# A two-layer streaming encoder step: the two MLPs begin in a fixed engine order, the up product runs by halves of the tokens

## The chip, the cores and the metric

The kernel runs on one core of a Trainium2 chip. The core has a matrix engine (TensorE, PE in the profile, with its weight loads as PEld), three engines for elementwise work (VectorE = DVE, ScalarE = ACT, GpSimd = POOL) and SyncE (SP), which here only issues DMAs. Each engine runs its own list of instructions in order and waits on semaphores. The metric is the device time of one execution in microseconds.

## The reference

Two layers run over 1072 tokens (16 meta, 32 sample and 1024 prompt tokens) of width 1024, in fp32. Layer 0 mixes by windowed attention and gated linear attention, layer 1 by forgetting attention; what matters here is the end of each layer:

```python
def rmsnorm(x, g):
    xf = x.astype(jnp.float32)
    y = xf * lax.rsqrt(jnp.mean(xf * xf, axis=-1, keepdims=True) + EPS)
    return (y * g.astype(jnp.float32)).astype(x.dtype)

def mlp(h, w_up, w_down):
    u = jax.nn.relu(h @ w_up)
    return (u * u) @ w_down
...
    xp = xp + mlp(rmsnorm(xp, norm_mlp[l]), w_up[l], w_down[l])
    xs = xs + mlp(rmsnorm(xs, norm_mlp[l]), w_up[l], w_down[l])
```

The hidden width is 4096, so w_up is 1024 x 4096 and w_down 4096 x 1024.

## The kernel before, in words

**Residual and products.** The residual stream stands transposed in SBUF: `xT` is [128, 8, 1072], feature block by token. It is cut into four quarters of tokens (268 wide in layer 0, 264 in layer 1). An fp32 product is done as three matmuls (`mm3`, L72 to L77): every operand is split by `hi_lo` (L62) into a high part, a cast on ScalarE (L64), and a low part, a subtraction on VectorE (L66). The mixer's output product (`add_product`, L823) adds 8 feature blocks of each quarter to `xT` (L833).

**Norm.** Beside these products `norm` squares the quarter on ScalarE (L134), adds the squares on VectorE and Pool (L136, L139), takes the column mean with one matmul by a constant matrix (L145) and forms the reciprocal root on ScalarE and VectorE (L148 to L152). `mlp_norm` (L867) scales `xT` by gain and root in 8 VectorE instructions (L873).

**MLP operands.** The up product is done with seven products in place of eight on 2 x 2 blocks. The blocks are B11, B21 (quarters 0 and 1, upper and lower features), B12, B22 (quarters 2 and 3) and the sums T1 to T4 (`mlp_sums`, L879), and each is split into `ho_B` or `ho_T` tiles. Halves c = 0 and 1 are the first and the second quarter of such a pair. The weights go by 16 column pairs b; for each, `up_load` (L899) fetches 1 MB of w_up into `mu_raw`, and `up_weights` (L907) forms the seven pieces A11 to S4 (`mu_w`).

**Up.** `up` (L932) runs, for each b, the seven pieces in the order of `UP` (L896), both halves with one piece: A11 with B11, A12 with B21, S1 with T1, S2 with T2, S3 with T3, A22 with T4, S4 with B22. One piece in one half is a step of 12 matmuls. The results are evicted into `xT`'s own memory (`xT` itself is first saved to `xsave` in HBM), squared, combined by four subtractions (L1000) and stored as `ud` by one DMA on SP's queue (L1001). Two areas of `xT` take turns, so pair b + 2 overwrites what pair b stored.

**Down.** `down` (L1010) runs seven passes in two halves over 16 blocks kb. It loads four 1 MB pieces of w_down (`md_k`, L1018) and reads `ud` back in pieces (`md_ur`, L1058), which are split into `md_w` and `md_u`. In the first pass `xT` is restored from `xsave` (L1102); one-element Pool copies (L1064) keep such loads from starting before a given activation piece has been read.

**Order.** In the MLP only TensorE's list is written by hand; VectorE, ScalarE, Pool and SP are ordered by a scheduler that follows a simulated timeline. Pools of tiles lie in two stacks, left and right; a tile that lies where an earlier one lay waits for that tile's last use.

## Time and profile before

| | us |
|---|---|
| median of three runs | 2867.91 (2854.82, 2867.91, 2869.13) |
| the profiled execution, first to last | 2855.66 |
| its span, first to last instruction | 2853.9 |
| mean granted clock of TensorE | 0.963 |
| layer 0: first product add to steady up matmuls | 559.5 to 646.6 |
| layer 0: last up matmul, first down matmul | 972.67, 986.29 |
| layer 1: first product add to steady up matmuls | 2091.5 to 2164.2 |
| layer 1: last up matmul, first down matmul | 2485.25, 2499.10 |

The times are taken from one profiled execution. A row of a timeline is start, duration, engine, line, operation, output<-inputs, shape, and in brackets the idle time ahead of it and what ended that. In a row of a group stand the number of instructions, busy time and mean duration. Durations of neighbours overlap by their start-up, so the distance between starts is the shorter and the truer cost.

### The profile page before, as it was taken

To read this page: it belongs to the slowest core of one execution; us is meant where nothing else is said; L and a number is where in the kernel's file an instruction comes from. 1 tells how busy PE (TensorE), PEld (TensorE's weight loads), DVE (VectorE), ACT (ScalarE), POOL (GpSimd) and SP (SyncE) were. 2 spreads that over 40 slices of the span, in tenths; PEclk is the share of its full clock that TensorE was granted. 3 is DMA by queue.
4 is the path that set the end of the run, shared out by engine and by line. 5 is a ranking of instruction groups with operands and counts; after the bars stand their busy time and mean duration, and the time that the engine had idled before them with its cause. 6 is when DMAs were issued, how large, how long until landed. Compare 5 with 4: busy or idle time off the path is not lost.

```text
span 2853.9 us, 49119 instructions
## 1 busy us (share of the span) xinstructions
PE 2631.2 (92%) x18391; PEld 2440.6 (86%) x18391; DVE 1888.3 (66%) x3856; ACT 1264.4 (44%) x2820; POOL 560.7 (20%) x611
## 2 busy tenths in 40 slices
PE   5899988879999899999999978999978999899998
PEld 5788966769999799999789856778768999899998
DVE  5934376687676677578643556778888666677553
ACT  4435454243333345445333346666653333335342
POOL 3423354200000010003110244555520000010000
PEclk9999988899999899999999979999988999999999
DMA  5343241143445577544465374344332444486643
GB/s 192 100 134 104 72 140 45 30 120 101 151 129 164 202 231 218 168 134 121 123 193 168 115 176 127 89 101 102 77 91 79 144 147 144 164 274 205 200 138 105
DMA packets 371286, 393.77 MB, mean 138 GB/s; under 512 B 41503, under 2 KB 300280, under 8 KB 369000
## 3 DMA queue, kind: packets, MB, share of 16 engines
q1 hardware_dynamic: 368552, 383.62, 45.6%
q0 software_dynamic: 2496, 7.01, 0.7%
q8 instruction: 145, 2.38, 0.4%
q14 instruction: 93, 0.76, 0.1%
HBM read 263.94 MB, written 125.48 MB: 136 GB/s over the span
## 4 chain that ended last, share of the span: by engine, by line
PE 63%; issue 16%; DVE 9%; DMA 3%; ACT 2%; SPq 1%; POOL 1%; DVEq 0%; ACTq 0%; POOLq 0%
PE bank L75 11%; PE bank L76 11%; PE bank L77 11%; PE mu_y L77 5%; PE mu_y L76 5%; PE mu_y L75 5%; PE bank L1470 2%; PE bank L1480 1%; PE bank L1481 1%; PE fx_s L1452 1%; PE fx_s L1453 1%; DMA md_raw<-in_w_down 1%; PE bank L257 1%; DVE gl_Q L600 1%; PE b L701 1%
## 5 line engine op out<-in xcount | busy, mean ns | idle before, releaser
L75 PE MATMUL bank<-pj_wh,h 128*128 128x384 f32 (+3 forms) x832 | 298.0, 360 | 9.4 <-ACT pj_wh L64 7.0
L77 PE MATMUL bank<-pj_wh,h 128*128 128x384 f32 (+3 forms) x832 | 295.9, 357 | 6.0 <-DVE h L66 4.8
L76 PE MATMUL bank<-pj_wl,h 128*128 128x384 f32 (+3 forms) x832 | 297.3, 358 | 3.5 <-DVE pj_wl L66 3.5
L75 PE MATMUL mu_y<-md_u,md_w 128*128 128x268 f32 (+1 forms) x896 | 259.4, 289 | 26.9 <-ACT md_u L64 26.9
L76 PE MATMUL mu_y<-md_u,md_w 128*128 128x268 f32 (+1 forms) x896 | 257.8, 288 | 2.4 <-DVE md_u L66 2.4
L77 PE MATMUL mu_y<-md_u,md_w 128*128 128x268 f32 (+1 forms) x896 | 257.3, 287 | 0.0
L75 PE MATMUL bank<-md_u,md_w 128*128 128x268 f32 (+1 forms) x896 | 257.1, 287 | 0.0
L77 PE MATMUL bank<-md_u,md_w 128*128 128x268 f32 (+1 forms) x896 | 255.2, 285 | 0.0
L76 PE MATMUL bank<-md_u,md_w 128*128 128x268 f32 (+1 forms) x896 | 254.9, 285 | 0.0
L64 ACT CAST md_u<-md_ur 128x536 fp32r<-128x536 f32 (+1 forms) x224 | 141.1, 635 | 210.7 <-PE mu_y L77 110.7
L66 DVE TENSOR_TENSOR md_u<-md_ur,md_u 128x536 fp32r<-128x536 f32 (+1 forms) x224 | 157.9, 710 | 114.2 <-ACT md_u L64 113.8
L76 PE MATMUL mu_y<-ho_T,mu_w 128*128 128x268 f32 (+1 forms) x768 | 219.8, 286 | 0.2 <-DVE ho_T L66 0.2
L77 PE MATMUL mu_y<-ho_T,mu_w 128*128 128x268 f32 (+1 forms) x768 | 219.9, 286 | 0.0
L75 PE MATMUL mu_y<-ho_T,mu_w 128*128 128x268 f32 (+1 forms) x768 | 219.2, 285 | 0.0
L75 PEld LDWEIGHTS mu_y<-md_u,md_w 128*128 128x128 f32 x896 | 171.1, 191 | 27.4 <-ACT md_u L64 27.3
L66 DVE TENSOR_TENSOR mu_w<-mu_raw,mu_w 128x512 fp32r<-128x512 f32 x160 | 110.0, 688 | 117.0 <-ACT mu_w L64 117.0
L1283 POOL TENSOR_TENSOR fx_p<-fx_p,sm_den 128x144 f32<-128x144 f32 (+7 forms) x128 | 150.6, 1177 | 181.8 <-DVE sm_den L1282 164.7
L64 ACT CAST mu_w<-mu_raw 128x512 fp32r<-128x512 f32 x160 | 99.2, 622 | 188.6 <-PE bank L77 124.6
L75 PEld LDWEIGHTS bank<-pj_wh,h 128*128 128x128 f32 x832 | 158.8, 191 | 22.3 <-ACT pj_wh L64 7.5
L76 PEld LDWEIGHTS mu_y<-md_u,md_w 128*128 128x128 f32 x896 | 170.9, 191 | 3.5 <-DVE md_u L66 3.4
L77 PEld LDWEIGHTS bank<-pj_wh,h 128*128 128x128 f32 x832 | 158.6, 191 | 17.5 <-DVE h L66 5.1
L76 PEld LDWEIGHTS bank<-pj_wl,h 128*128 128x128 f32 x832 | 159.0, 191 | 16.3 <-DVE pj_wl L66 5.2
(538 smaller groups left out, 8096.2 us busy)
## 6 DMA issues: line engine op xcount, KB each, us to landing
md_raw<-in_w_down SPq DMA_DIRECT2D x160, 256.0 KB
mu_raw<-in_w_up SPq DMA_DIRECT2D x64, 512.0 KB
ud<-xT SPq DMA_DIRECT2D x16, 1876.0 KB
md_ur<-ud SPq DMA_DIRECT2D x112, 268.0 KB
ud<-xT SPq DMA_DIRECT2D x16, 1848.0 KB
md_ur<-ud SPq DMA_DIRECT2D x112, 264.0 KB
md_k<-in_w_down SPq DMA_DIRECT2D x16, 1024.0 KB
fh_ka<-zk SPq DMA_DIRECT2D x32, 260.0 KB
```

What stands on the lines that cost most here:

```text
L64: nc.scalar.copy(hi, src)
L66: nc.vector.tensor_tensor(lo, src, hi.bitcast(F32), op=ALU.subtract)
L75: mm(out, ah, bh, start=start, stop=False)
L76: mm(out, ah, bl, start=False, stop=False)
L77: mm(out, al, bh, start=False, stop=stop)
L257: nc.tensor.matmul(*args, start=k == x == 0, stop=k == KB - 1 and x == 1)
L600: eng.tensor_tensor(ov, xv[r, :, :, 1], qv[r, :, :, 1], op=ALU.mult)
L701: nc.tensor.matmul(po[:m, h % 2, h // 2], att[:, h, :m], v[:, P * h:P * h + P], start=True, stop=False)
L1283: nc.gpsimd.tensor_tensor(p[:, :n], p[:, :n], den[:, 0:1].to_broadcast([P, n]), op=ALU.mult)
L1452: nc.tensor.matmul(s[:, a:b], qa[:, qc], ka[:, t0 + a:t0 + b], start=True, stop=False)
L1453: nc.tensor.matmul(s[:, a:b], qb[:, qc], kb[:, t0 + a:t0 + b], start=False, stop=ma >= mb)
L1470: nc.tensor.transpose(pt[:m, P * j:P * j + P], pr[j][:, k0:k0 + m], self.ident)
```

## The change

**Begin of the MLP.** `mlp_start` replaces `norm`, `mlp_norm` and `mlp_sums` for the MLPs. It writes out one order for TensorE, VectorE and ScalarE (`in_order`): after each product it squares the block on ScalarE, saves two blocks at a time, and lets `beside` emit queued work (weights, scalings, operand forms) until a budget of estimated us is used. The square sums are halved by two pair additions a quarter, and the column sums are accumulated by TensorE (two matmuls after each). `xT` is scaled by the root alone, in two instructions of four blocks; the gains go into the up weights (`up_gain`, ScalarE).

**Up.** The 32 units (b, c) follow each other in an order that interleaves two units. `mlp_first` emits its first steps in the fixed order too, until the last operand is formed; behind that only TensorE's list is fixed. Evictions use strided places in `xT`; A22's square goes from VectorE to ScalarE; the `ud` store goes from SP's queue to Pool's.

**Down.** The first w_down load and the first activations come ahead of the other loads, six weights are formed ahead instead of sixteen, and the pools are cut finer.

**Memory.** The stacks of many tiles change sides, so that operands and weights of the MLP lie where they wait for other tiles than before. In `scaled`, the norm of the few first rows takes two `nm_t` tiles in place of one `lx_t` tile, a buffer that the loads of x use as well.

```diff
+            for k0 in range(0, KB, 4):
+                t0 = sb.tile([P, w], F32, name="nm_t", bufs=bufs)[:, :4 * few].rearrange("p (k f) -> p k f", f=few)
+                for k in range(4):
+                    nc.vector.scalar_tensor_tensor(t0[:, k], x[:, k0 + k, :few], self.gain[:, n, k0 + k:k0 + k + 1], y[:, :few], op0=ALU.mult, op1=ALU.mult)
+                self.hi_lo(t0, h[:, k0:k0 + 4, 0:few], h[:, k0:k0 + 4, 64:64 + few])
...
+        self.up_pool = pool
+        self.operands("ho1", [(x, c) for c in range(2) for x in ("B11", "B21")])
+        self.nst = pool("nst")
+        self.operands("ho2", [(x, 0) for x in ("T2", "T1", "T3")])
+        self.mua = pool("mua")
...
+        self.scales = 0
+        self.raw0, self.w0 = self.up_load(0, self.mua), {}
+        for k in range(0, KB, 2):
+            self.work.append((0.4, lambda k=k: [self.up_gain(self.raw0, k + j) for j in range(2)], None))
+        for x in ("A11", "A12", "S1", "S2", "S3"):
+            self.work.append((1.0, partial(self.up_weights, x, self.raw0, self.w0), None))
...
+    def in_order(self):
+        return self.tc.manual_schedule(engines={mybir.EngineType.PE, mybir.EngineType.DVE, mybir.EngineType.Activation})
...
+    def beside(self, us):
+        self.step += 1
+        for f in self.due.pop(self.step, ()):
+            f()
+        while self.work and us > 0 and self.work[0][2] in (None, *self.ho):
+            t, f, _ = self.work.popleft()
+            f()
+            us -= t
+    def later(self, steps, f):
+        self.due.setdefault(self.step + steps, []).append(f)
...
+        def form(q, y):
+            c0, c1 = self.qs[q]
+            x1, x2 = (self.xT[:, k:k + 4, c0:c1] for k in (0, 4))
+            yb = y.unsqueeze(1).to_broadcast([P, 4, qw])
+            def scale(x, *then):
+                def go():
+                    self.scales -= 1
+                    tt(x, x, yb, op=ALU.mult)
+                    for name in then:
+                        hi(name, x, q)
+                return 1.25, go, None
+            def low(name, x):
+                return 1.25, lambda: lo(name, x, q), (name, q % 2)
+            def sub(dst, a, b, name=None):
+                def go():
+                    tt(dst, a, b, op=ALU.subtract)
+                    if name:
+                        hi(name, dst, q)
+                    else:
+                        self.formed.add(("free", q))
+                return 1.25, go, None
+            def high(name, x):
+                return 0.0, lambda: hi(name, x, q), (name, q % 2)
+            if q < 2:
+                return [scale(x1, "B11"), scale(x2, "B21"), low("B11", x1), low("B21", x2)]
+            a0, a1 = self.qs[q - 2]
+            b11, b21 = (self.xT[:, k:k + 4, a0:a1] for k in (0, 4))
+            return [scale(x1), sub(b11, x1, b11, "T1"), scale(x2), low("T1", b11), sub(b11, x2, b11, "T2"), sub(x1, x2, x1, "T3"),
+                    low("T2", b11), sub(b21, b21, b11), low("T3", x1), high("T4", b21), high("B22", x2), low("T4", b21), low("B22", x2)]
+        sums, pairs = {}, {}
+        def column_sums(q, n):
+            if n == 0:
...
+                sums[q] = self.ps.tile([P, 512], F32, name="mu_y")
+            sq = pairs.pop((q, n))
+            for j in range(2):
+                nc.tensor.matmul(sums[q][:, :qw], self.mean, sq[:, j], start=n == j == 0, stop=n == j == 1)
+        def row(q):
+            ps = sums.pop(q)
+            while self.scales:
+                self.work.popleft()[1]()
+            y, a = (sb.tile([P, QMAX], F32, name=f"ns_{x}")[:, :qw] for x in "ya")
+            nc.scalar.activation(a, ps[:, :qw], AF.Ln, bias=self.eps)
+            nc.scalar.activation(y, a, AF.Exp, scale=-0.5)
+            nc.scalar.activation(a, y, AF.Square)
+            def finish():
+                nc.vector.scalar_tensor_tensor(a, ps[:, :qw], EPS, a, op0=ALU.add, op1=ALU.mult)
+                nc.vector.scalar_tensor_tensor(y, a, -3.0, y, op0=ALU.add, op1=ALU.mult)
+                self.work.extend(form(q, y))
+                self.scales = 2
+            self.later(1, finish)
+        for q in range(4):
+            c0, c1 = self.qs[q]
+            for ob in range(KB):
+                product(q, ob)
+                n = ob // 4
+                if ob % 4 == 0:
+                    sq = []
+                if ob % 2 == 0:
+                    sq.append(sb.tile([P, 2, QMAX], F32, name=f"ns_q{len(sq)}", bufs=2 - len(sq))[:, :, :qw])
+                nc.scalar.activation(sq[ob % 4 // 2][:, ob % 2], self.xT[:, ob, c0:c1], AF.Square)
+                if ob % 2:
+                    nc.sync.dma_start(self.xsave[:, ob - 1:ob + 1, c0:c1], self.xT[:, ob - 1:ob + 1, c0:c1])
+                if ob % 4 == 3:
+                    pairs[q, n] = sq[0]
+                    self.later(2, lambda a=sq[0], b=sq[1]: tt(a, a, b, op=ALU.add))
+                    self.later(3, partial(column_sums, q, n))
+                    if n:
+                        self.later(3, partial(row, q))
+                self.beside(us)
...
+    def up_load(self, b, pool):
+        raw = pool.tile([P, KB, 2, P], F32, name=f"mu_raw{b % 2}", bufs=1)
...
             self.nc.sync.dma_start(raw[:, :, h], wu[:, :, h, P * b:P * b + P])
...
+    def up_gain(self, w, k):
+        x = w["raw"][:, k]
+        self.nc.scalar.mul(x, x, self.gain[:, 2 * self.l + 1, k:k + 1])
...
+        units = [(b, c) for b in range(self.NP) for c in range(2)]
+        order = [(0, "A11"), (0, "A12"), (0, "S2"), (0, "S1"), (0, "S3")]
+        for u in range(len(units)):
+            late = [(u + 1, "A11"), (u, "A22"), (u + 1, "A12"), (u, "S4"), (u + 1, "S2"), (u + 1, "S1"), (u + 1, "S3")]
+            order += [x for x in late if x[0] < len(units)]
...
-        def ready(at):
-            for b, n in todo[at:at + 4]:
-                if (b, n) not in ws:
-                    if b not in pairs:
-                        pairs[b] = {"raw": self.up_load(b, sb)}
-                    ws[b, n] = self.up_weights(self.UP[n][0], pairs[b], sb)
...
+        raws, ws, pr = {0: self.raw0}, {0: self.w0}, {}
+        def load(b):
+            raws[b] = self.up_load(b, self.mub if b % 2 else self.mua)
+        load(1)
+        for u, wn in order:
+            b, c = units[u]
+            yield 1.2, ((self.UP[wn], c), wn)
+            w = ws[b][wn]
+            at = self.qs[2 * (b % 2)][0]
...
+            if c:
+                def squared(x):
+                    stt(v[x], v[x], 0.0, v[x], op0=ALU.max, op1=ALU.mult)
+                if wn == "A12":
+                    squared("B11")
...
+                    squared("B22")
                 elif wn == "A22":
-                    nc.scalar.activation(u["B21"], out, AF.Relu)
+                    nc.scalar.activation(v["B21"], v["B21"], AF.Square)
                 elif wn == "S4":
-                    tt(u["B12"], u["B12"], out, op=ALU.add)
...
-            elif wn == "S4":
-                squared(v["B12"], v["B12"])
-                for x, p, m in (("T1", "B12", "B11"), ("T2", "B22", "T1"), ("T3", "B22", "B12"), ("T4", "B21", "T2")):
-                    tt(v[x], v[p], v[m], op=ALU.subtract)
-                nc.sync.dma_start(self.ud[b // 4][:, b % 4], place[:, b % 2, 1:8, :hw])
...
+                    squared("B12")
+                    for x, p, m in (("T1", "B12", "B11"), ("T2", "B22", "T1"), ("T3", "B22", "B12"), ("T4", "B21", "T2")):
+                        tt(v[x], v[p], v[m], op=ALU.subtract)
+                    nc.gpsimd.dma_start(self.ud[b // 4][:, b % 4], place[:, 1:8])
...
+                if b + 1 < self.NP:
+                    if wn == "A11":
+                        ws[b + 1] = {}
+                        for k in range(KB):
+                            self.up_gain(raws[b + 1], k)
+                    for x in {"S2": (), "S1": ("S1", "S2")}.get(wn, (wn,)):
+                        self.up_weights(x, raws[b + 1], ws[b + 1])
...
-        for kb in range(NP):
+        load(k1[0], "A11", 0, 4)
+        ready(0)
+        for x in range(1, 4):
+            load(k1[x], "A11", 4 * x, 4)
+        for kb in range(6):
             w[0, kb] = weights(0, kb)
...
+                if n == 0 and c == 0 and kb + 6 < NP:
+                    w[0, kb + 6] = weights(0, kb + 6)
...
+                ks = ExitStack()
+                kp = pool(ks, "mk", "right")
...
+                k2, k1 = ([kp.tile([P, 4, 512], F32, name=f"md_k{x}{y}") for y in range(4)][::-1] for x in (2, 1))
+                if self.l:
+                    self.so = pool(st, "so", "left", 2)
+                sb = {x: pool(st, f"md{x}") for x in ("u", 0, 1, 2, 3, "raw")}
...
+    def mlp_first(self):
+        self.operands("ho3", [(x, 1) for x in ("B22", "T4", "T3", "T1", "T2")] + [(x, 0) for x in ("B22", "T4")], "right")
+        self.mub = self.up_pool("mub", "right")
+        for x in ("A22", "S4"):
+            self.work.append((1.0, partial(self.up_weights, x, self.raw0, self.w0), None))
+        self.steps = self.up()
+        for us, wants in self.steps:
+            while not all(x in self.formed or x in self.w0 for x in wants):
+                self.beside(0.1)
+            if us:
+                self.beside(us)
+            if ("B22", 1) in self.formed and not self.work:
+                break
...
-            norm()
+            first.close()
...
-            steps = [[partial(product, q, ob) for ob in range(KB)] for q in range(4)]
-            for q in range(4):
-                while steps[q]:
-                    steps[q].pop(0)()
-                self.spill(q)
-                if q < 3:
-                    self.mlp_norm(q, [steps[q + 1].pop(0) for _ in range(3)])
+            with self.in_order():
+                self.mlp_begin(1)
+                self.mlp_start(product, 1.5)
+        with self.in_order():
+            self.mlp_first()
...
+            for n in range(2):
+                load(n)
+            for n in range(2):
+                split(n)
...
+                C.mlp_start(product, 1.0)
+        with C.in_order():
+            C.mlp_first()
```

VectorE's list in layer 1, quarter 3, from the last root of the norm to the operands; before (`ho_T_2381x` and `ho_B_23815` are operands with both halves in one tile):

```order
L152 SCALAR_TENSOR_TENSOR nm_y<-nm_a,nm_y 128x264
L873 SCALAR_TENSOR_TENSOR xT<-xT,gain,nm_y 128x264 x8
L884 TENSOR_TENSOR xT<-xT 128x4x264
L66 TENSOR_TENSOR ho_B_23815<-xT,ho_B_23815 128x4x264
L888 TENSOR_TENSOR xT<-xT 128x4x264
L66 TENSOR_TENSOR ho_T_23811<-xT,ho_T_23811 128x4x264
L66 TENSOR_TENSOR ho_T_23813<-xT,ho_T_23813 128x4x264
L886 TENSOR_TENSOR xT<-xT 128x4x264
L890 TENSOR_TENSOR xT<-xT 128x4x264
L66 TENSOR_TENSOR ho_T_23812<-xT,ho_T_23812 128x4x264
```

Here the products are over; the scalings are eight instructions with the gain, and all forms follow. After, the same place in quarter 2, where the last products run (L827 adds a product to `xT`, L977 adds a pair of squares):

```order
L958 SCALAR_TENSOR_TENSOR ns_y<-ns_a,ns_y 128x264
L911 TENSOR_TENSOR xT<-xT,ns_y 128x4x264
L921 TENSOR_TENSOR xT<-xT 128x4x264
L827 TENSOR_TENSOR xT<-xT,bank 128x264
L911 TENSOR_TENSOR xT<-xT,ns_y 128x4x264
L900 TENSOR_TENSOR ho_T_23557<-xT,ho_T_23557 128x1056
L827 TENSOR_TENSOR xT<-xT,bank 128x264
L977 TENSOR_TENSOR ns_q_23885<-ns_q_23885,ns_q_23913 128x2x264
L921 TENSOR_TENSOR xT<-xT 128x4x264 x2
L827 TENSOR_TENSOR xT<-xT,bank 128x264
L900 TENSOR_TENSOR ho_T_23556<-xT,ho_T_23556 128x1056
```

The scalings are two instructions of four blocks each, the forms stand between product adds, and the first T operands have tiles of one half.

SP's list at layer 0's change from up to down, before (`mu_raw` is the last up weights, `ud` the store, `md_k` the first w_down loads, `md_ur` the activations):

```order
L903 DMA mu_raw<-in_w_up 128x8x128 x2
L1001 DMA ud_6543<-xT 128x3752 x2
L1018 DMA md_k_10197<-in_w_down 128x4x512
L1018 DMA md_k_10198<-in_w_down 128x4x512
L1018 DMA md_k_10199<-in_w_down 128x4x512
L1018 DMA md_k_10200<-in_w_down 128x4x512
L1058 DMA md_ur<-ud_6540 128x2x268 x2
L1058 DMA md_ur<-ud_6541 128x2x268
```

The w_down loads stand ahead of the activations and behind a `ud` store. After:

```order
L992 DMA mu_raw_9829<-in_w_up 128x8x128 x2
L1163 DMA md_ur<-ud_6546 128x2x268 x2
L1163 DMA md_ur<-ud_6547 128x2x268 x2
L1163 DMA md_ur<-ud_6548 128x2x268
L1211 DMA xT<-xsave_5941 128x2x268 x2
L1163 DMA md_ur<-ud_6548 128x2x268
L1123 DMA md_k_10319<-in_w_down 128x4x512
L1123 DMA md_k_10318<-in_w_down 128x4x512
```

The activations and the first restore of `xT` stand ahead of the w_down loads, and the `ud` store is no longer in SP's list.

312 lines of the change are left out of this document (127 added, 185 removed).

## The prediction

> **What bounds the kernel now.** I read the page's busy line first, then the waits of TensorE, then the windows around the two longest waits, then the timeline there.
>
> ```profile
> PE 2631.2 (92%) x18391; PEld 2440.6 (86%) x18391; DVE 1888.3 (66%) x3856; ACT 1264.4 (44%) x2820; POOL 560.7 (20%) x611
> PE mu_y L75 <- ACT md_u L64: 26.9, 2, 13.6
> PE bank L75 <- ACT ho_T L64: 22.1, 2, 11.6
> 2163.80:2485.50 321.70, 321.70 (x2627) 321.53 (x2627) 221.40 (x383) 109.22 (x233) 0.00 (x0) 0.99 0.43 133
> 643.70:972.80 329.10, 326.94 (x2628) 326.35 (x2628) 225.85 (x386) 110.67 (x234) 0.00 (x0) 0.99 0.41 131
> 2091.50:2163.80 72.30, 39.05 (x252) 36.64 (x251) 65.02 (x126) 34.64 (x65) 9.02 (x8) 0.80 0.35 104
> 559.50:643.70 84.20, 61.52 (x440) 57.45 (x438) 70.09 (x133) 39.06 (x74) 7.91 (x8) 0.92 0.40 118
> ```
>
> The window rows give bounds, length, then busy PE, PEld, DVE, ACT, POOL, clock, DMA share, GB/s. TensorE is busy 92%, so only its idle time and its slow clock can be won. The two steady up stages (321.7 and 329.1 us) are TensorE alone, with VectorE a third idle; nothing in the change shortens them. Two waits, each met once in each layer, make 49 us: the start of the down stage (md_u) and the last operands of the up stage (ho_T). Ahead of the second the bound is VectorE: from layer 1's first product add (2091.5) to the start of steady matmuls (2163.8) it works 65.0 of 72.3 us, TensorE 39.
>
> ```profile
> 972.55 0.29 PE L76 MATMUL bank<-ho_B,mu_w 128*128 128x268 f32 x1
> 972.67 0.29 PE L77 MATMUL bank<-ho_B,mu_w 128*128 128x268 f32 x1
> 986.29 0.59 PE L75 MATMUL mu_y<-md_u,md_w 128*128 128x268 f32 x1 [13.34 <-ACT md_u L64]
> 2161.32 0.59 PE L75 MATMUL bank<-ho_T,mu_w 128*128 128x264 f32 x1 [10.52 <-ACT ho_T L64]
> 2164.17 0.42 PE L77 MATMUL bank<-ho_T,mu_w 128*128 128x264 f32 x1
> 2164.39 0.42 PE L75 MATMUL bank<-ho_T,mu_w 128*128 128x264 f32 x1
> 640.00:650.00 10.00, 4.37 (x18) 4.06 (x19) 10.00 (x12) 4.63 (x5) 0.00 (x0) 0.50 0.07 17
> ```
>
> Steady matmuls start 0.12 us apart. After a stall they start 0.22 apart, and the granted clock is 0.50 there (last row). So a step of the up stage, 12 matmuls, is 12 x 0.12 = 1.45 us.
>
> **The begin of the MLP.** Before, layer 1's VectorE work in the 72.3 us is mostly in these groups (busy and mean count overlap; the timeline gives the spacing).
>
> ```profile
> L873 DVE SCALAR_TENSOR_TENSOR xT<-xT,gain,nm_y 128x264 f32<-128x264 f32 x32 | 13.6, 494 | 0.0
> L833 DVE TENSOR_TENSOR xT<-xT,bank 128x264 f32<-128x264 f32 x32 | 13.0, 422 | 5.3 <-PE bank L77 5.2
> L66 DVE TENSOR_TENSOR ho_T<-xT,ho_T 128x1056 fp32r<-128x1056 f32 x6 | 7.5, 1250 | 0.0
> L136 DVE TENSOR_TENSOR nm_acc<-nm_acc,nm_t 128x264 f32<-128x264 f32 x16 | 7.0, 437 | 2.3 <-ACT nm_acc L134 2.2
> 2155.67 3.32 DVE L873 SCALAR_TENSOR_TENSOR xT<-xT,gain,nm_y 128x264 f32<-128x264 f32 x8
> 2162.47 2.48 DVE L66 TENSOR_TENSOR ho_T<-xT,ho_T 128x1056 fp32r<-128x1056 f32 x2
> 974.22 2.72 DVE L1000 TENSOR_TENSOR xT<-xT 128x536 f32<-128x536 f32 x4
> L139 DVE TENSOR_TENSOR nm_acc<-nm_acc,nm_acc 128x264 f32<-128x264 f32 x4 | 1.7, 429 | 0.2
> ```
>
> The change takes 32 scalings with the gain out (eight take 3.32 us, so 13.3) and puts 8 multiplies of 1056 columns in. The nearest shape is the subtraction of 1056 columns, two in 2.48 us, 1.2 each, so 9.6. It takes out 16 + 4 square additions (7.0 + 1.7, about 7.4 after overlap) and puts in 8 pair additions of 528 columns (four of 536 take 2.72, 0.68 each, so 5.4). One low part less (1.2) and one subtraction more (1.2) stand ahead of the operand that TensorE waits for. Sum: 13.3 - 9.6 + 7.4 - 5.4 = 5.7, about 6 us less of VectorE. The gains now cost 8 ScalarE multiplies of 128x256 per column pair, and the squares stay on ScalarE, which is busy only 34.6 of these 72.3 us. In the first pair, though, they wait for the weight load and stand ahead of squares in a fixed order; with the load on time this costs nothing, late up to 5 us. The mean matmuls rise from 4 to 16:
>
> ```profile
> L145 PE MATMUL bank<-nm_acc,mean 128*128 128x264 f32 x8 | 3.8, 569 | 10.6 <-DVE nm_acc L139 10.6
> ```
>
> That is 0.95 us a quarter at most, so 12 more cost up to 11.4, on a TensorE idle 33 us of this window; its cover goes only if VectorE falls below 50 us here.
>
> I take VectorE's idle time as before, 7.3 us (72.3 - 65.0): 59 + 7.3 = 66.3, so the awaited operand comes 6 us earlier. Also, TensorE has more to do ahead of it: before, 5 steps (A11 and A12 in both halves, S1 of the first) lie ahead of the awaited operand; in the new order 9 (A11, A12, S2, S1, S3 of half 0, then A11 of half 1, A22, A12, S4). Four steps x 1.45 = 5.8 us. Against it stands what VectorE still owes when steady work begins: T1, T3, T4 and B22 low parts of half 1 (four of 1.2 us) and the weights of the second pair, about 8 us of work beside 7 steps; I take 3 us of new waits. **Layer 1: 6 + 5.8 - 3 = 9 us**, bounds 0 (engines in fixed orders stall each other) and 18 (VectorE without idle time: 7.3 more, and 3 us of waits less). In layer 0 the same VectorE work goes, its 14.1 us of idle time (84.2 - 70.1) belongs to waits for the op_ weights and stays: **9 us**, bounds 0 and 18.
>
> **From up to down.** The chain before:
>
> ```profile
> 970.03 3.88 SPq L1018 DMA_DIRECT2D md_k<-in_w_down  x4
> 975.36 2.18 ACT L64 CAST md_w<-md_k 128x512 fp32r<-128x512 f32 x4 [4.93 <-DMA md_k<-in_w_down]
> 983.53 2.18 ACT L64 CAST md_w<-md_k 128x512 fp32r<-128x512 f32 x4 [0.57 <-DMA md_k<-in_w_down]
> 985.61 1.71 ACT L64 CAST md_u<-md_ur 128x536 fp32r<-128x536 f32 x3
> ```
>
> Loads issue at 970.03, the first lands 5.3 us later, sixteen casts follow at the pace of the four loads (first and last group of four shown), and only behind them the cast of md_u that TensorE waits for: 13.3 us. After, the md_u casts stand on ScalarE ahead of the md_w casts, and their loads go out while the up stage still runs. Then the first matmul needs only the first md_k load. On SP it now stands behind the restore xT<-xsave, which waits for Pool copies of the third md_u, cast behind the last S3 eviction, two steps (2.9 us) before the up stage's end; with that cast, the copies and the issues the load goes out at about +0.5 to 1. Landing 5.3 and one cast 0.55 give a first matmul at +6.7 in place of +13.4. **Gain 6.7 in each layer, 13.4 in both**; bounds 0 and 26.
>
> **The ud store on the Pool queue.** It must have read xT before pair b+2 writes there: 11 steps x 1.45 = 16 us, less 3.5 us of VectorE (the square and four subtractions, the 2.72 row above): 12.5 us.
>
> ```profile
> 668.59 0.34 SPq L1001 DMA_DIRECT2D ud<-xT  x1
> 669.54 2.33 SPq L903 DMA_DIRECT2D mu_raw<-in_w_up  x2
> 678.00:680.00 2.00, 2.00 (x18) 2.00 (x17) 1.20 (x2) 0.44 (x2) 0.00 (x0) 1.00 0.27 66
> 680.00:682.00 2.00, 2.00 (x19) 2.00 (x18) 1.62 (x4) 0.86 (x2) 0.00 (x0) 1.00 0.00 0
> q0 software_dynamic: 2496, 7.01, 0.7%
> ud<-xT SPq DMA_DIRECT2D x16, 1876.0 KB
> L391 POOL DMA_DIRECT2D zb<-sw_z x36 | 20.4, 566 | 55.6 <-ACT sw_z L387 35.9 <-ACT sw_es L458 12.4 <-ACT sw_z L390 7.3
> ```
>
> The last row gives 0.57 us per issue on Pool. The store waits for the last subtraction; behind it on Pool's queue stand only the next stores and, at the end, the 1x1 copies. A late store would hold A11's eviction on ScalarE, and behind that the next casts of weights and TensorE's bank. On SP, store and weights are through by about 679, 10 us after the issue. Pool's own queue moved 7.01 MB in 0.7% of the span, 20 us, so 5.4 us for 1.88 MB. No row shows a Pool store of this size: below is 6 us, above some 14; I take 9, near the SP store, so it hides. The issues themselves hide on a Pool that is idle in both steady windows.
>
> [...]
>
> **The rest.** Up: ScalarE gains 8 multiplies and a square per pair, and VectorE loses that square, on engines idle for 212 and 100 us of 321.7: 0. At the start of the program few-row norm pieces take other buffers, so the second chunk no longer waits for the first's:
>
> ```profile
> 0.00:200.00 200.00, 158.64 (x885) 146.32 (x886) 129.04 (x344) 83.05 (x237) 70.59 (x71) 0.96 0.50 146
> ```
>
> Of TensorE's 41 us lost there I take 2 (bounds -3 and 6). Mixer B's first loads now share memory with mixer A's work buffers: -2 (bounds -5 and 0).
>
> **Sum.** 9 + 9 + 13.4 + 2 - 2 = 31.4 us. The profiled execution took 2855.66 us, so it would be 2824; the median of the three runs lies 12.25 higher, and half of this is added, because the runs lie at both ends of these 12 us: **2830**.
>
> **Rivals.**
> 1. *Slower.* The Pool store takes over 12.5 us. Then A11's eviction in pair b+2 waits, its bank is held, and TensorE stops. It decides from 12.5 us, and every us above it costs 14 pairs x 2 layers = 28 us. At 14.5 us: 2830 + 56 = 2886. For it: nothing of this size went through that queue. Against: 7.01 MB in 20 us. Chance 0.12.
> 2. *The begins give nothing.* VectorE's fixed order waits for TensorE and back, as it did for 5.2 us at L833, at each of the 8 norm rows. 2830 + 18 = 2848. Chance 0.18.
> 3. *The transitions give nothing*, since the load goes out only after the restore and the restore waits for the late b = 14 store: 2830 + 13 = 2843. Chance 0.12.
> 4. *The transitions vanish*, the load landing before the end: 2830 - 13 = 2817. Chance 0.10.
> 5. *Clock.* About 28 matmuls run at 0.22 in place of 0.12 after each stall, 2.8 us, and I leave this in all four places. If the two ho_T stalls become short, the slow clock goes too: 2830 - 6 = 2824. Chance 0.08, inside my range. [...]
>
> **How the numbers follow.** The forecast, 2814 to 2846, has 0.40. The bounds of the terms add up to 68 us of gain (18 + 18 + 26 + 6) and 8 of loss, from 2862 (2855.7 and the 6): 2794 to 2870. All at one end is unlikely; the range 2797 to 2868 leaves out most of rival 1 and little else. A measurement of this kernel tells from no change some 0.5%, 14 us, so "faster" is below 2853.6. Forecast, rivals 3, 4, 5 and half of 2 are there: 0.40 + 0.12 + 0.10 + 0.08 + 0.09 = 0.79; same 0.10; slower 0.11.
>
> **What would show it.** Right: the waits for ho_T and md_u fall to some 3 and 7 us; from layer 1's first product add to the T2 operand 66 us or so; the steady stages stay at 0.12 a matmul. Wrong: A11's eviction waits for a ud DMA; TensorE waits in the up stage every 20 us; product adds on VectorE wait behind forms and the products stretch; the first md_k load lands over 8 us after the up stage.

## The result, and the profile after

| | before | after |
|---|---|---|
| median, us (6 runs each) | 2867.73 (2854.82 to 2869.13) | 2883.86 (2877.41 to 2887.31) |
| ratio to before, 95% interval | | 1.0067 (1.0044 to 1.0091) |
| span of the profiled execution | 2853.9 | 2875.6 |

The forecast was 2830 us, in a range up to 2868. The kernel became 0.67% slower. The profiled executions lie 12 and 6 us under their kernels' medians, so the stages below differ by 21.7 us in all where the medians differ by 16.1. First the busy line of the changed kernel, and those of TensorE's waits that lie in the MLPs (us in total, times, longest):

```profile
PE 2650.5 (92%) x18439; PEld 2457.6 (85%) x18439; DVE 1868.9 (65%) x3754; ACT 1380.3 (48%) x3110; POOL 582.4 (20%) x627
PE mu_y L945 <- DVE ns_q L977: 38.9, 14, 11.6
PE mu_y L76 <- ACT md_w L65: 17.3, 2, 9.1
PE mu_y L76 <- ACT xT L1073: 15.6, 5, 9.4
PE mu_y L76 <- ACT md_u L65: 9.9, 2, 6.1
```

VectorE has less to do (1868.9 us against 1888.3), and the old wait at the start of the down stage is smaller. The top row of the waits is new: the mean matmul (L945) waits 38.9 us for the pair additions of squares (L977), 31.8 of them in layer 1. The row of L1073 is in the main the step of T2: the operand is ready, but TensorE's bank is freed last, by ScalarE's eviction (9.4 us in layer 0, 4.8 in layer 1).

The stages by the trace, from the starts of matmuls and operand instructions. "Begin" reaches from the first output product of the MLP (mixb in layer 0, the first one of 264 columns in layer 1) to the low part of the last T operand, "layer" from the same first product to the last up matmul, "down" from there to the last down matmul. A begin is a part of its layer, so it has no difference of its own in the sum:

| us | before | after | difference |
|---|---|---|---|
| up to layer 0's first product | 557.3 | 553.4 | -3.9 |
| layer 0: begin | 94.8 | 98.6 | |
| layer 0: first product to last up matmul | 415.4 | 417.1 | +1.7 |
| layer 0: down (of it until its first matmul) | 351.8 (13.6) | 353.0 (8.6) | +1.2 |
| layer 1's mixer | 765.6 | 762.8 | -2.8 |
| layer 1: begin | 79.6 | 101.7 | |
| layer 1: first product to last up matmul | 395.2 | 415.6 | +20.4 |
| layer 1: down (of it until its first matmul) | 360.3 (13.8) | 365.3 (9.4) | +5.0 |
| end | 8.3 | 8.4 | +0.1 |

The differences add up to the 21.7 us between the spans. How far such a number can be read is shown by the experiments below, which share the changed kernel's code in most stages: the way to layer 0's first product took them 547.7 to 558.7 us, layer 1's mixer 762.7 to 767.6, the down stages 353.0 to 357.5 and 358.9 to 366.8 (without e10, which leaves out loads there). Begins with the same code repeat within 1.5 us. Of the kernel before there is one profile. So one thing is clear of this scatter at a glance: layer 1's begin, 22.1 us longer. Layer 0's is 3.8 longer, and the rest of that layer gives 2.1 of it back.

The windows of the two begins (before and after, layer 0 and layer 1 each; columns as in the prediction):

```profile
557.30:652.10 94.80, 69.96 (x481) 65.36 (x480) 79.66 (x143) 43.76 (x80) 7.91 (x8) 0.89 0.36 105
2090.10:2169.70 79.60, 46.35 (x290) 43.94 (x289) 71.70 (x133) 37.59 (x69) 9.02 (x8) 0.79 0.32 94
```

```profile
553.40:652.00 98.60, 77.07 (x549) 72.14 (x548) 72.28 (x105) 54.46 (x108) 0.00 (x0) 0.95 0.30 91
2086.30:2188.00 101.70, 61.72 (x359) 56.84 (x357) 64.90 (x96) 48.47 (x97) 0.00 (x0) 0.82 0.22 68
```

VectorE's work fell by 7.4 and 6.8 us. Its idle time rose from 15.1 to 26.3 us in layer 0 (94.8 - 79.7; 98.6 - 72.3) and from 7.9 to 36.8 us in layer 1.

How it idles is seen in one half quarter (four of the eight products of a quarter) of layer 1, on VectorE and on TensorE's mean matmul (start, duration, then in brackets the idle time and what ended it):

```profile
2114.95 2.42 DVE L900 TENSOR_TENSOR ho_B<-xT,ho_B 128x1056 fp32r<-128x1056 f32 x2
2117.29 0.42 DVE L827 TENSOR_TENSOR xT<-xT,bank 128x264 f32<-128x264 f32 x1
2117.63 0.70 DVE L977 TENSOR_TENSOR ns_q<-ns_q,ns_q 128x528 f32<-128x528 f32 x1
2118.25 0.42 DVE L827 TENSOR_TENSOR xT<-xT,bank 128x264 f32<-128x264 f32 x1
2121.87 0.43 DVE L827 TENSOR_TENSOR xT<-xT,bank 128x264 f32<-128x264 f32 x1 [3.20 <-PE bank L78]
```

```profile
2118.39 2.12 PE L945 MATMUL mu_y<-ns_q,mean 128*128 128x264 f32 x4 [5.59 <-DVE ns_q L977]
2125.13 1.16 PE L945 MATMUL mu_y<-ns_q,mean 128*128 128x264 f32 x4 [0.41 <-DVE ns_q L977]
```

In VectorE's written list the pair addition (L977) stands behind two low parts (L900). TensorE reaches the mean matmul early and waits 5.59 us; the next product stands behind it. When the pair addition is done, VectorE has one product left to add, and then waits 3.20 us for the mean matmul (2.12 us) and the product behind it. Each engine waits for the other in turn.

### The profile page after: what moved, and what is told of

It reads as the page before. It is cut to its first block, busy times and chain, and to the rows that moved or that the text cites. A ratio compares the mean times of both kernels' runs of the same rounds, so it can differ in the third digit from the quotient of the medians.

```text
span 2875.6 us, 49327 instructions
## 1 busy us (share of the span) xinstructions
PE 2650.5 (92%) x18439; PEld 2457.6 (85%) x18439; DVE 1868.9 (65%) x3754; ACT 1380.3 (48%) x3110; POOL 582.4 (20%) x627
## 5 line engine op out<-in xcount | busy, mean ns | idle before, releaser
L76 PE MATMUL bank<-pj_wh,h 128*128 128x384 f32 (+3 forms) x832 | 296.0, 358 | 12.5 <-ACT h L65 4.2
L76 PEld LDWEIGHTS mu_y<-md_u,md_w 128*128 128x128 f32 x896 | 172.7, 193 | 28.1 <-ACT md_w L65 17.8
L1100 POOL DMA_DIRECT2D ud<-xT x32 | 31.7, 991 | 810.2 <-ACT xT L1079 294.0
L77 PEld LDWEIGHTS mu_y<-md_u,md_w 128*128 128x128 f32 x896 | 172.6, 193 | 3.9 <-DVE md_u L67 3.7
L78 PEld LDWEIGHTS mu_y<-md_u,md_w 128*128 128x128 f32 x896 | 172.2, 192 | 0.4 <-DVE md_w L67 0.4
L76 PEld LDWEIGHTS bank<-md_u,md_w 128*128 128x128 f32 x896 | 168.8, 188 | 0.1
L77 PEld LDWEIGHTS bank<-pj_wl,h 128*128 128x128 f32 x832 | 158.1, 190 | 12.5 <-DVE pj_wl L67 1.3
L77 PEld LDWEIGHTS bank<-md_u,md_w 128*128 128x128 f32 x896 | 168.7, 188 | 0.1
L78 PEld LDWEIGHTS bank<-md_u,md_w 128*128 128x128 f32 x896 | 168.6, 188 | 0.0
```

Of the source, the lines that this page charges most:

```text
L76: mm(out, ah, bh, start=start, stop=False)
L77: mm(out, ah, bl, start=False, stop=False)
L78: mm(out, al, bh, start=False, stop=stop)
L1100: nc.gpsimd.dma_start(self.ud[b // 4][:, b % 4], place[:, 1:8])
```

## The experiments

The edits are to the changed kernel, those of e13, e14 and e16 to e11's. The kernel before, run beside each group on the same chip, took 2863.0 us (e1 to e4), 2862.3 (e5 to e8), 2862.9 (e9 to e12), 2855.3 (e13 to e15) and 2865.6 (e16 and e17, median of nine). Stages are of one profile each; the times are single runs but for the first two rows and e17 (median of five). A list is called fixed where the program writes its order out, free where the scheduler orders it along its simulated timeline. Measured values (us; begin and layer as above):

| run | begin 0 | layer 0 | down 0 | begin 1 | layer 1 | down 1 | time |
|---|---|---|---|---|---|---|---|
| before | 94.8 | 415.4 | 351.8 | 79.6 | 395.2 | 360.3 | 2867.7 |
| changed | 98.6 | 417.1 | 353.0 | 101.7 | 415.6 | 365.3 | 2883.9 |
| e1_ahead | 101.0 | 419.8 | 356.5 | 99.0 | 413.2 | 366.8 | 2882.3 |
| e2_free | 103.1 | 425.0 | 354.0 | 83.4 | 401.0 | 363.2 | 2867.8 |
| e3_long | 95.8 | 437.0 | 354.5 | 99.7 | 438.3 | 359.5 | 2917.4 |
| e4_down | 99.7 | 418.2 | 354.8 | 101.7 | 415.9 | 364.0 | 2881.4 |
| e5_urq | 99.6 | 417.7 | 357.5 | 102.0 | 417.0 | 364.1 | 2885.3 |
| e6_sp | 99.8 | 418.3 | 353.7 | 101.9 | 416.2 | 360.5 | 2882.3 |
| e7_fix | 104.5 | 422.7 | 354.2 | 88.2 | 403.3 | 359.7 | 2869.1 |
| e8_l1free | 99.7 | 417.8 | 354.5 | 85.6 | 403.9 | 362.3 | 2873.5 |
| e9_nogain | 97.2 | 416.3 | 354.1 | 100.7 | 414.8 | 365.4 | 2885.5 |
| e10_k2 | 99.4 | 417.4 | 348.8 | 101.3 | 415.4 | 357.5 | 2860.6 |
| e11_best | 100.8 | 418.6 | 354.4 | 74.3 | 391.2 | 361.7 | 2858.2 |
| e12_dvefree | 105.2 | 422.7 | 354.6 | 94.5 | 409.3 | 363.8 | 2877.3 |
| e13_b16 | 109.0 | 426.9 | 354.4 | 74.2 | 391.7 | 361.5 | 2864.0 |
| e14_b24 | 109.5 | 427.4 | 353.5 | 75.8 | 394.0 | 365.5 | 2870.1 |
| e15_allfree | 95.0 | 416.6 | 354.7 | 75.9 | 394.1 | 358.9 | 2858.8 |
| e16_b06 | 100.8 | 418.7 | 354.3 | 75.1 | 393.6 | 359.7 | 2858.7 |
| e17_best | 100.7 | 418.8 | 354.8 | 74.3 | 391.5 | 361.3 | 2856.6 |

**Who waits in the begin.** e1 lets TensorE run two products ahead of VectorE's additions:

```diff
-                product(q, ob)
+                while ahead and len(held) < 3:
+                    self.adds = []
+                    product(*ahead.pop(0))
+                    held.append(self.adds)
+                    self.adds = None
+                for add in held.popleft():
+                    add()
```

> Edit to the changed kernel: TensorE issues each product of the MLP's begin two products ahead of the VectorE addition that empties it; all other orders stay. Theory A (lockstep): in layer 1 TensorE's mean matmul stands in front of products and waits for a pair addition (31.8 us in 8 waits), and VectorE's next product addition waits for those products (18.6 us in 13). Then both waits shrink, to under 15 and under 6 us, and layer 1's stretch from the first product add of 264 columns (2088.0) to the low part of T2 of the second half (2180.0), 92 us, falls to 75 to 80; the whole time falls by 12 to 17 us, layer 0 by at most 3 of it. Theory B (the added work itself: 12 more fp32 mean matmuls, gains, saves): the stretch stays over 88 us and the time within 3 us.

Theory A holds in the mean's wait (under 15 us), nearly in the wait for products (9.2 against 6), and falls in stretch and time. In layer 1:

```profile
PE bank L76 <- DVE xT L827: 16.2, 5, 4.2
PE mu_y L948 <- DVE ns_q L987: 11.5, 5, 4.0
DVE xT L827 <- PE bank L78: 9.2, 7, 2.6
DVE ns_a L960 <- ACT ns_a L957: 7.9, 3, 2.6
```

The mean's wait fell from 31.8 to 11.5 us, and in its place TensorE waits 16.2 us for banks that VectorE has not emptied, and VectorE 7.9 us for the root's row on ScalarE. To the low part of T2 it was 89.4 us (2093.8 to 2183.2) instead of 92. Taking one wait out of three fixed lists moved it. Stretch and time are those that theory B gave, but its cause, the added work, is not it: e2 below keeps that work, and its stretch is 15 us shorter.

e2 frees VectorE's and ScalarE's lists:

```diff
-        return self.tc.manual_schedule(engines={mybir.EngineType.PE, mybir.EngineType.DVE, mybir.EngineType.Activation})
+        return self.tc.manual_schedule(engines={mybir.EngineType.PE})
```

> Edit to the changed kernel: in the MLP's begin only TensorE's list is fixed; VectorE and ScalarE are ordered by the scheduler, as before the change. Theory A (the fixed order of VectorE and ScalarE is what stalls): the stretch of layer 1, 92 us, comes back to 72 to 80, and the time falls by 10 to 20 us. Theory B (TensorE's own list, with the mean matmuls three products behind, is what stalls): TensorE's waits for the pair additions stay over 20 us and the time within 6 us.

Layer 1's begin fell from 101.7 to 83.4 us, and to T2 it took 77.3 (2095.1 to 2172.4), inside what theory A said; the time fell by 16 us. TensorE still waited 19.6 us for pair additions there, close to theory B's bound, so a part of the wait belongs to its own list. Layer 0 took 8 us longer, which neither theory said.

e12 frees VectorE alone:

```diff
-        return self.tc.manual_schedule(engines={mybir.EngineType.PE, mybir.EngineType.DVE, mybir.EngineType.Activation})
+        return self.tc.manual_schedule(engines={mybir.EngineType.PE, mybir.EngineType.Activation})
```

> Edit to the changed kernel: TensorE and ScalarE keep the fixed order, VectorE is ordered by the scheduler. Theory A (VectorE's fixed list does the harm in layer 1): the stretch of 101.7 us falls to 82 to 88, as with both free (83.4). Theory B (ScalarE's fixed list, with squares ahead of casts and roots, does it): it stays over 95.

94.5 us lies between the two, half a us under theory B's bound: freeing VectorE alone brings 7.2 of the 18.3 us that freeing both brings. ScalarE alone was not freed. e3 makes the fixed order longer (`at_unit` is the unit of the step):

```diff
-            if ("B22", 1) in self.formed and not self.work:
+            if ("B22", 1) in self.formed and not self.work and us and self.at_unit > 4:
```

> Edit to the changed kernel: the fixed order lasts four units longer, so that the gain multiplies of the third column pair cannot stand in ScalarE's list ahead of the last operands' high parts. Theory A: there they wait 2.3 us for a load and take 3.3 us, 5.5 us on the path to T2 in each layer; the waits for T2 and the A11 eviction (9.4 us in layer 0, 4.8 in layer 1) fall by 4 to 5.5 each and the time by 8 to 11 us. Theory B (VectorE sets T2's time anyway): the time within 3 us.

Both theories fall: the time grew by 33.5 us. The begins changed by 2 to 3 us, but the further steps in fixed order cost some 20 us in each layer (437.0 and 438.3 against 417.1 and 415.6). The new rows among TensorE's waits are evictions on ScalarE, which in its fixed list stand behind weight casts and gain multiplies that wait for VectorE:

```profile
PE mu_y L76 <- ACT xT L1078: 26.1, 11, 4.7
PE mu_y L76 <- ACT xT L1080: 11.3, 9, 3.8
```

The question of the gain multiplies was put again in e9, which leaves them out for the third pair:

```diff
-                        for k in range(KB):
+                        for k in range(KB if b != 1 else 0):
```

> Edit to the changed kernel: the gain multiplies of the third column pair are left out (its up product then lacks the gain), which in the changed kernel stand in ScalarE's list ahead of the high parts of the last T operands. Theory A (they wait 2.3 us for a load and take 3.3 us, and this is on the path): the stretch from the first product to the last T low part falls from 98.6 and 101.7 us by 4 to 6 in each layer, the time by 8 to 12. Theory B (VectorE's own list sets T2): under 2 us in each layer.

1.4 and 1.0 us in the begins: theory B. VectorE's list ends last here: in layer 1 of e9 its subtraction behind T2's low part ends at 2189.16, and the eviction that frees TensorE's bank for the step of T2 starts at 2189.32; in layer 0 the same eviction starts at 649.33, after 1.75 us of waiting for that subtraction.

**Repairing it.** e7 keeps all lists fixed and shortens three hand-overs; besides e1's edit:

```diff
-                    self.later(2, lambda a=sq[0], b=sq[1]: tt(a, a, b, op=ALU.add))
+                    def fold(a=sq[0], b=sq[1]):
+                        tt(a, a, b, op=ALU.add)
+                        tt(a[:, 0], a[:, 0], a[:, 1], op=ALU.add)
+                    self.later(2, fold)
...
-            self.later(1, finish)
+            self.later(3, finish)
...
-                self.beside(us)
+                self.beside(us if q or ob > 5 else 0)
```

The mean is then one matmul a half, over `sq[:, 0]`.

> Edit to the changed kernel, keeping the fixed order: products two ahead on TensorE (as in the first run), the pair sums folded once more on VectorE so that one mean matmul a half replaces two, the last two steps of the norm's root two products later, and the first weights begun after six products. Theory A (three serial hand-overs a quarter, mean matmul 2.1 us, root row 2.6 us wait, weight load 5 us at the start, make VectorE idle 33 us in layer 1): the stretch from layer 1's first product matmul to the start of the last T low part (101.7 us, and 99.0 with the first edit alone) falls to 80 to 88. Theory B (in fixed lists the waits only move): over 93.

88.2 us in layer 1, just outside theory A's span and far from theory B's, and 6 us more in layer 0's begin. So written lists need not cost all this: with shorter hand-overs they give back 13.5 of the 22.1 us. e8 frees layer 1 alone and folds the sums as e7 does:

```diff
+    def in_order(self, l=0):
+        more = () if l else (mybir.EngineType.DVE, mybir.EngineType.Activation)
+        return self.tc.manual_schedule(engines={mybir.EngineType.PE, *more})
...
-            with self.in_order():
+            with self.in_order(1):
```

> Edit to the changed kernel: in layer 1 only TensorE's list is fixed (as in the second run, which had it in both layers), layer 0 stays fixed; and one mean matmul a half replaces two, with one more VectorE addition. Theory A: layer 1 takes 401 us or less from the first product to the last up matmul (415.6 in the changed kernel, 401.0 in the second run), layer 0 stays at 417 +- 3, and the time falls by 14 to 20 us. Theory B (layer 1's gain in the second run came from where layer 0 left it): layer 1 stays over 408.

Layer 0 stayed. Layer 1 took 403.9, between the two bounds and near theory A's: most of what e2 gained in layer 1 is layer 1's own, and folding the sums brought nothing on top. The time fell by 10 us, less than said. e11 puts e1's edit, the folded sums and the free lists of layer 1 together:

> Edit to the changed kernel: layer 1 with only TensorE's list fixed, products two ahead, one mean matmul a half. Theory A (what is left in layer 1 is TensorE's wait for pair additions, 19.6 us in the second run): the stretch from the first product to the last T low part falls under 80 us (83.4 in the second run, 79.6 before the change), the first product to the last up matmul to 393 to 398. Theory B (the stretch is at VectorE's limit, 65 us of work and the root's chain): 82 to 87.

```profile
2095.20:2169.50 74.30, 51.78 (x317) 49.59 (x316) 68.09 (x106) 47.68 (x95) 0.00 (x0) 0.79 0.30 92
DVE xT L827 <- PE bank L78: 3.2, 8, 0.8
```

Theory A: VectorE works 68.1 of 74.3 us, as busy as before the change, and waits 3.2 us in place of 18.6 for products. Its idle time is 6.2 us, so the 28.9 us that the change had added are gone. The layer's 391.2 us are 2 better than theory A's span: 24 us shorter than in the changed kernel and 4 shorter than before the change (the six profiles with this code in layer 1 took 391.2 to 394.1). From e8, e11 differs by e1's edit alone: running two products ahead brings 11.3 us with free lists (85.6 to 74.3) and 2.7 with fixed ones (101.7 to 99.0). And e11 keeps the rest of the change, the gains in the weights, the forms, the order of units and the places in memory, so none of these explains layer 1's loss. This version was timed again:

> The kernel of e11_best once more, timed. Theory A (layer 1's begin is repaired and 4 us shorter than before the change, all other stages within 3 us of before): ratio to the kernel before 0.996 to 1.000. Theory B (other stages, the down stages of 354 and 362 us against 352 and 360, cost what layer 1 gains): 1.000 to 1.003.

Ratio to the kernel before 0.9963 (0.9949 to 0.9976; 2856.57 against 2865.63 us): 0.4% faster than the kernel before, in theory A's range, and clearly faster than the changed one. Where these 9 us come from the stages do not show: e17's profile is of the longest of its five runs and before's of one of its shortest, and by them layer 0 and its down stage are 3 us longer each, layer 1 is 4 shorter.

**Layer 0.** Its begin was tried with more and with less queued work beside each product:

```diff
-                C.mlp_start(product, 1.0)
+                C.mlp_start(product, 1.6)
```

> Edit to the run e11_best: in layer 0 the fixed order puts 1.6 us of queued work beside each product in place of 1.0. Theory A (the tail of layer 0 is VectorE work that the budget of 1.0 left over while VectorE idled beside the products): the stretch from the first product to the last T low part falls from 100.8 us to 92 to 96 and the first product to the last up matmul from 418.6 to 410 to 414. Theory B (the tail is the last quarter's own chain): within 2.5 us.

> Edit to the run e11_best: in layer 0 the fixed order puts 2.4 us of queued work beside each product in place of 1.0. Theory A: as with 1.6 or better, 88 to 95 us and 406 to 413. Theory B (more work beside the products holds up the additions that TensorE's banks wait for): the products stretch by as much as the tail shrinks, within 2.5 us of 100.8 and 418.6.

> Edit to the run e11_best: in layer 0 the fixed order puts 0.6 us of queued work beside each product in place of 1.0. Theory A (in VectorE's fixed list queued work ahead of a product addition holds up TensorE's bank, so less of it is better, as 1.6 and 2.4 were worse): the products end earlier than the 62.7 us of e11_best by 2 or more, the stretch to the last T low part is 100.8 or less and the whole layer stays under 418. Theory B (1.0 is where TensorE and VectorE balance; what is not done beside the products is done behind them): the products end earlier, but the stretch to the last T low part grows by 3 us or more.

1.6 and 2.4 made the begin 8 us longer, against both theories in both runs. 0.6 changed nothing: the products took 63.0 us and the begin 100.8, as in e11, so neither theory holds there either. But it is hardly a test: `beside` compares the budget before it emits an item, and a form counts as 1.25, so 0.6 and 1.0 both let one form through beside a product (1.6 and 2.4 both let two). From the first quarter's root on, VectorE's list in e16 is e11's but for one swap of neighbours. With VectorE's and ScalarE's lists free in both layers, and e11's other edits:

> Edit to the changed kernel: only TensorE's list fixed in both layers, products two ahead, one mean matmul a half. Theory A (fixed lists hurt layer 0 as they hurt layer 1): layer 0 falls under 412 from the first product to the last up matmul (417.1 changed, 418.6 in e11_best). Theory B (layer 0's products are bound by TensorE, and a fixed order does not hurt there): 417 to 426, layer 1 as in e11_best (391 +- 3).

416.6 and 394.1: theory B, within half a us of its bounds. No run brought layer 0 under the 415.4 us of before; the best take 416 to 419. What its products cost is seen in part in the rows of the mean matmul in the product stage, before and after (553.4 to 619.5, before 557.3 to 615.2):

```profile
L145 PE MATMUL bank<-nm_acc,mean 128*128 128x268 f32 x6 | 1.9, 406 | 1.4 <-DVE nm_acc L139 1.4
```

```profile
L945 PE MATMUL mu_y<-ns_q,mean 128*128 128x268 f32 x28 | 8.0, 408 | 6.1 <-DVE ns_q L977 6.1
```

6.1 us more work and 4.7 us more waiting on an engine that is busy 57 of these 66 us: the products end 8.2 us later, and the shorter tail behind them pays 6.5 of that back. The means are not all of it: in e15 they work 4.8 us and wait for nothing, and the products still take 62.3 us against 57.9 before. Which wait would have to go for layer 0 to fall under 415 was not found.

**From up to down.** e4 takes the loads and weights back to the old order, e5 issues the activations' loads from ScalarE's queue, e10 replaces 4 MB of loads by zeros (the down product then lacks that part):

```diff
-        load(k1[0], "A11", 0, 4)
-        ready(0)
-        for x in range(1, 4):
+        for x in range(4):
             load(k1[x], "A11", 4 * x, 4)
-        for kb in range(6):
+        for kb in range(NP):
             w[0, kb] = weights(0, kb)
...
```

> Edit to the changed kernel: the down stage's loads and weights in the order of before the change (four w_down loads, sixteen weights, then the first activations). Theory A (the DMA engines are the bound for the first 40 us of the down stage, share 1.0 in both kernels, so an earlier start is paid back by later waits): the gap from the last up to the first down matmul grows from 7.3 and 8.1 us to 12 to 15, and the time from the last up to the last down matmul (351.6 and 363.8 us) stays within 3 us in each layer, 6 in all. Theory B (the shorter gap is a real gain): the time grows by 10 to 14 us.

The gap is 9.1 us in both layers (8.6 and 9.4 in the changed kernel by the starts used here, where the expectation has 7.3 and 8.1): the scheduler orders these queues, and at layer 0's change SP's list has the same loads in the same order as without the edit, so this run tells the theories apart in nothing.

```diff
-            nc.sync.dma_start(t, self.ud[g // 2][:, 2 * (g % 2):2 * (g % 2) + 2, s, qw * c:qw * c + qw])
+            nc.scalar.dma_start(t, self.ud[g // 2][:, 2 * (g % 2):2 * (g % 2) + 2, s, qw * c:qw * c + qw])
```

> Edit to the changed kernel: the down stage's activation loads (md_ur) are issued from ScalarE's queue, so they no longer stand behind w_down loads in SP's list. Theory A (the order of SP's list makes the later md_u late): the waits for md_u inside the first pass (3.8 and 6.1 us) go, and the time from the last up to the last down matmul falls from 353.0 and 365.3 us by 4 to 8 in each layer. Theory B (the DMA engines, share 1.0, are the bound there): another load becomes late instead and both times stay within 2.5 us.

No gain: md_u's low part was waited for instead (5.3 and 5.6 us). In layer 0 it stands in VectorE's list behind work that waits 2.67 us for another w_down load, as theory B has it. 357.5 in layer 0 is 2 us beyond theory B's bound on the other side.

```diff
-                    behind(x[0:1, 0, 0:1], u)
-                    load(x, "A21", kb - 2, 4)
+                    nc.gpsimd.memset(x, 0.0)
```

> Edit to the changed kernel: the second 4 MB of w_down in each layer (the k2 pieces, 10 us of all DMA engines at 400 GB/s) are not loaded; Pool fills them with zeros, so the down product is another one. Theory A (DMA is the bound of the first 40 us of the down stage): the waits inside the first pass (md_u, 3.8 and 6.1 us) go, the first matmul comes earlier than 8.6 and 9.4 us after the up stage, and the time from the last up to the last down matmul falls from 353 to 357 and 360 to 367 us to 343 to 349 and 351 to 357. Theory B (order of issue or ScalarE and VectorE bound it): these times stay within 3 us of 353 and 363.

The down stages fell to 348.8 and 357.5 us, by 4 and 8: one in theory A's span, one half a us above it. They are 4.2 and 1.4 under the shortest of the runs that load everything, so the second alone would show little. The windows of the first pass, changed kernel and e10, at the same distance from the last up matmul (970.5 and 965.1):

```profile
981.00:991.00 10.00, 10.00 (x75) 10.00 (x74) 4.76 (x8) 4.55 (x9) 0.00 (x0) 0.89 1.04 412
991.00:1001.00 10.00, 10.00 (x82) 9.92 (x81) 7.06 (x13) 3.71 (x7) 1.36 (x1) 1.00 1.05 378
1001.00:1011.00 10.00, 5.12 (x29) 4.70 (x28) 9.32 (x16) 1.92 (x3) 0.18 (x1) 0.83 0.99 315
```

```profile
975.60:985.60 10.00, 10.00 (x76) 10.00 (x76) 5.58 (x9) 4.69 (x9) 0.00 (x0) 0.91 1.03 397
985.60:995.60 10.00, 9.56 (x78) 9.35 (x77) 9.81 (x17) 2.98 (x7) 0.00 (x0) 1.00 0.62 202
995.60:1005.60 10.00, 9.55 (x77) 9.34 (x76) 10.00 (x19) 5.35 (x9) 1.25 (x4) 1.00 0.96 307
```

In the changed kernel the share stays at 1.0 and TensorE stops at 1002 us, for 3.8 us, until md_u is there; with 4 MB less it does not, and in layer 1 the 6.1 us wait for md_u is gone as well. e5 has moved the order of issue without gain, so the bytes are the better explanation. The first matmul came hardly earlier in e10 (7.7 and 9.6 us behind the last up matmul, 8.6 and 9.4 in the changed kernel), so that part of theory A fell.

**The store on Pool's queue.**

```diff
-                    nc.gpsimd.dma_start(self.ud[b // 4][:, b % 4], place[:, 1:8])
+                    nc.sync.dma_start(self.ud[b // 4][:, b % 4], place[:, 1:8])
```

> Edit to the changed kernel: the ud store is issued from SP's queue, as before the change. Theory A (the Pool queue carries the store as well as SP does; its landing of 7.7 us is under the 12.5 us it has): the up stages from the last T operand on and the time stay within 4 us. [...]

Theory A: 2882.3 us against 2883.9 in the changed kernel, the same within the scatter.

## Why the prediction was wrong

**The step that failed** is "I take VectorE's idle time as before, 7.3 us (72.3 - 65.0): 59 + 7.3 = 66.3, so the awaited operand comes 6 us earlier". On the same stretch, from the first product add to the end of T2's low part, the changed kernel has in layer 0 and layer 1:

```profile
555.40:644.05 88.65, 70.55 (x510) 65.83 (x508) 66.63 (x99) 46.80 (x92) 0.00 (x0) 0.97 0.33 101
2087.97:2180.05 92.08, 55.55 (x320) 50.89 (x318) 59.47 (x88) 41.62 (x82) 0.00 (x0) 0.81 0.22 70
```

In layer 1 VectorE's work came out as worked out, 59.5 us for 59. Its idle time is 32.6 us in place of 7.3 (in layer 0 22.0 in place of 14.1), so the stretch took 92 us and not 66. The idle time is not a property of the work. Before, the scheduler had laid VectorE's and ScalarE's lists beside TensorE's along its timeline; in the three lists as written out here, VectorE and TensorE wait for each other in turn, and the prediction's own sign of being wrong, product adds that wait behind forms, is in the timeline above. e2 brought the stretch to T2 to 77.3 us by freeing two lists, e11 the begin to 74.3.

**What it weighs.** Between the profiled executions 31.4 us less were forecast and 21.7 more measured, 53.1 us apart. Layer 1 accounts for 29.4 (9 less forecast, 20.4 more measured), layer 0 for 10.7 (9 less, 1.7 more), the two down stages for 19.6 (13.4 less, 6.2 more); the start and layer 1's mixer came out 6.7 better than forecast.

**The bound of that term** was wrong with it: "0 (engines in fixed orders stall each other)" let the stall at worst undo the gain. Rival 2 named the mechanism, VectorE's fixed order waiting for TensorE and back, and priced it at 18 us, the gain undone; in layer 1 alone it cost the 9 us of gain and 20.4 us more. Nothing in the profile of before bounded it. The lists of the changed kernel might have, had one quarter been followed through all three engines (two low parts, then the pair addition, then the mean, then the product that the next addition needs); no run tests that. The upper bound was off by little: 9 + 7.3 + 3 is 19.3, where it says 18.

**The cover "on a TensorE idle 33 us of this window"** did not hold for the mean matmuls. Idle time covers work only where that work can run when the engine is idle; here it stood in the list ahead of products. In layer 0, where TensorE is busy 57 of 66 us beside the products, 6.1 us of further mean work had little room, which the prediction had not looked at: it took layer 0's gain over from layer 1. Why layer 0's products take longer is shown in part only (e15 above), and that part of the miss stays open.

**"Four steps x 1.45 = 5.8 us"** less 3 for new waits was right in size: from the first matmul with the awaited operand to the last up matmul it took 329.0 and 324.0 us before (from 643.73 and 2161.32), 324.7 and 320.1 after (from 645.83 and 2181.80), 4.3 and 3.9 us less against 2.8. That matmul came 6.0 and 24.3 us later behind the first product, in place of 6 earlier.

**"Gain 6.7 in each layer, 13.4 in both"**: the gap to the first down matmul fell by 5.0 and 4.4 us, to 8.6 and 9.4. Its chain in layer 0:

```profile
971.14 14.43 SPq L1123 DMA_DIRECT2D md_k<-in_w_down  x6
978.40 2.19 ACT L65 CAST md_w<-md_k 128x512 fp32r<-128x512 f32 x4 [7.98 <-DMA md_k<-in_w_down]
983.60 2.19 ACT L65 CAST md_w<-md_k 128x512 fp32r<-128x512 f32 x4 [3.01 <-DMA md_k<-in_w_down]
```

The first load took 7.3 us from issue instead of 5.3, and the next came 5.2 us behind it, where before they followed at 2.7. No end came earlier: within the pass md_u is late by 3.8 and 6.1 us (the last row of the waits above). The DMA engines were as full before the change as after (share in the last but one column):

```profile
986.00:996.00 10.00, 9.24 (x54) 8.94 (x55) 3.45 (x7) 1.48 (x4) 1.94 (x5) 0.70 1.05 396
996.00:1006.00 10.00, 9.69 (x78) 9.47 (x77) 9.03 (x15) 2.42 (x4) 0.90 (x2) 1.00 1.07 382
```

With e10, these rows make the DMA engines the likely bound of the stage's start, so an earlier first matmul only moves the wait. The prediction followed ScalarE's casts and did not read this column.

**The store** hid as forecast: it lands in 7.7 us (median) where 9 were taken and 12.5 are free. All land within 9.1 us but the last of each layer (13.0 and 13.2), whose memory no later pair overwrites, and no instruction of the up stage waited for one.

```profile
ud<-xT POOLq DMA_DIRECT2D x16, 1876.0 KB, 7.7
```

Rival 1, on which the forecast's chance of "slower" lay, did not happen; that its 2886 us are close to the measured time is luck. In the up stage (700 to 950 us) VectorE was busy 171.8 of 250 us beside these stores, and those issued there landed in 7.1 to 9.1 us, under the 12.5 that are free.

**The steady up stage** was unchanged as forecast, eight multiplies a pair on ScalarE and all. Before and after, 700 to 950 us:

```profile
700.00:950.00 250.00, 250.00 (x2030) 250.00 (x2029) 172.75 (x301) 84.92 (x182) 0.00 (x0) 1.00 0.44 140
```

```profile
700.00:950.00 250.00, 250.00 (x2028) 250.00 (x2027) 171.76 (x290) 125.22 (x282) 11.86 (x12) 1.00 0.41 140
```

The start (-3.9) and layer 1's mixer (-2.8) lie within the scatter of runs that share their code; nothing can be said of "2" and "-2".

## What to carry to other kernels

When several engines get lists written out by hand, cost the hand-overs and not only the work: walk one period of the loop through all lists and add up each wait for another engine, since the engine that was 90% busy in the scheduler's lists (71.7 of 79.6 us) was 64% busy in the written ones (64.9 of 101.7). Give the engine that feeds the others room to run ahead, and leave to the scheduler the lists whose order you do not need; here it took both to win the stretch back in full. Before counting an earlier start as a gain, read the DMA share of the stretch that follows: where it was 1.0 here, the earlier start only moved the wait.
